# Looking up the experts' numbers with 16-bit operands, the positions spread out by ScalarE

## The chip, the cores and the metric
The kernel runs on one core of a Trainium2 chip. The time is device microseconds of one launch. [...] The engines are called PE (TensorE), DVE (VectorE), ACT (ScalarE), POOL (GpSimd) and SP (SyncE).

## The reference, cut to what matters
The layer mixes 512 latent tokens (with 256 context tokens) in an S5 group and a Hyena group, and then sends every token through PEER, an expert layer with 16384 experts that are single neurons (a row of `peer_u` and a row of `peer_v`, 1024 long). All is float32. The part of PEER that the change is in:

```python
s1, s2 = q1 @ k1.T, q2 @ k2.T            # per token and head: 128 scores each
v1, i1 = lax.top_k(s1, 16)
v2, i2 = lax.top_k(s2, 16)
cand = v1[..., :, None] + v2[..., None, :]        # 256 pairs
sc, ci = lax.top_k(cand.reshape(..., 256), 16)    # 8 heads, 16 experts a token
e = i1[ci // 16] * 128 + i2[ci % 16]              # the experts' numbers
g = softmax(sc)
act = gelu(u[e] . h)
out = sum(g * act * v[e])
```

Only 50 of the 256 pairs can be among the best 16 of a head; the kernel forms those, in a list padded to 54, with their sums `cand` and the experts' numbers `cid` beside one another.

## The kernel before, in words
Tokens are 4 blocks of 128 (`lt` 0 to 3), one token a partition. The tokens of block 0 are served by gathering their experts' rows (`gathered`, L1430 to L1439: an indirect DMA on POOL, a dot product `junk` on DVE, a gelu of one column on ACT, L1434, its product with the gate on ACT, L1436, and a weighted sum `accg` on DVE). The 384 tokens of the other blocks go through all experts as matmuls: 128 u-blocks of 128 experts (`first`: 24 matmuls of 128x384, then a gelu `ga`, stored to `GA` in DRAM, L1380) and 128 v-blocks (`second`, 18 matmuls of 128x512 into `pacc`), each weighted by a matrix of gates `GD` that is built by one-hot matmuls (`gates`, L1560). Each float32 matmul is three: an operand is split into a high part (`h`, a copy on ACT, L302, L1611, L1620) and a low part (`l`, raw minus high on DVE, L303, L1612, L1621), and L307, L308, L309 multiply high by high, low by high and high by low.

The stages after the mixers, by the trace's time:

- **Heads**, 500 to 806 us. For each of 8 heads: two query blocks `wq` (24 matmuls of 128x512 each), scores against the keys, the best 16 of both halves (`top16`), and `pairs`: the list of 54 pairs, the best 16 of them (their places in the list are `pos`), and the look-up of their experts' numbers. Between these PE does u-blocks, 6.3 a head (`run_ahead`).
- **Transition**, 806 to 832 us: the softmax over all heads, `columns` (the numbers split into two indices, transposed by PE into `ptr`, L1505 to L1507, copied by ACT into `cols`, L1514 and L1515), and `gx2`, a vector spread over partitions: eight diagonal matrices `dg` (ACT, L1573, two buffers), each multiplied by ones on PE (`pgx`, L1574).
- **Gates**, 832 to 1055 us: one-hot matrices `o` (DVE L1551, ACT L1555 and L1556), their product on PE (`pgg`), a copy to `gst` (ACT, L1562). Gathers and u-blocks lie between.
- **Last stage**, 1055 us to the end: `second` for block after block. For block i ACT makes `vh` (L1611) and `wwh` (L1620), DVE `vl` (L1612), the weights `gw` (L1617) and `wwl` (L1621). `vh`, `vl`, `wwh` and `wwl` have three buffers each, so `wwh` of block i can be written only when PE is done with block i - 3. The 37 last u-blocks and the gathers lie between.

The look-up before, per head and token block: DVE compares each of the 16 positions with the 54 numbers 0 to 53 (`eq`, 16 x 54 = 864 float32 elements a partition, L1416), multiplies by `cid` (L1417) and sums over the 54 (L1418) into `EID`.

The order of the instructions on each engine is not written out: a scheduler with a model of the durations sets it for the whole program, so that a shorter instruction in one place moves others, also in later stages. Each engine then runs its queue in that order and waits where an operand isn't there.

Of the kernel before, what the change touches and what calls it, by code (L numbers as in the profile page):

```python
# [11 lines left out]
I32 = mybir.dt.int32  # L12
BF16 = mybir.dt.bfloat16
U32 = mybir.dt.uint32
AF = mybir.ActivationFunctionType
ALU = mybir.AluOpType
AX = mybir.AxisListType

P = 128
# [74 lines left out]
RGATE = 0  # L94
PERHEAD = 0
GH = 2.0
NOO = 3
S5M = 1
HYAT = 2
# [5 lines left out]
NCAND = 54 if MERGE else 50  # L105
# [123 lines left out]
def build(tc, I, out, dbg=None, stop=None):  # L229
# [58 lines left out]
    def b2(name, shape, dtype=F32):  # L288
        return cur[0].tile(shape, dtype, tag="b2", name=name, bufs=nb2[0])
# [4 lines left out]
    def sm(name, shape, dtype=F32, bufs=1, tag=None):  # L294
        return cur[0].tile(shape, dtype, tag=tag or name, name=name, bufs=bufs)

    def wblock(src, name, lo_eng=None):
# [3 lines left out]
        lo = wp.tile([P, D], F32R, tag="wl", name=name + "l")  # L301
        nc.scalar.activation(hi, raw, AF.Copy)  # L302
        (lo_eng or (nc.vector if FQ else nc.gpsimd)).tensor_tensor(lo, raw, hi.bitcast(F32), ALU.subtract)  # L303
# [30 lines left out]
    V = nc.vector  # L334
    A = nc.scalar
# [83 lines left out]
    sc = cp.tile([P, 8, 2], F32, tag="sc", name="sc")  # L419
    A.activation(sc, ccs, AF.Silu)  # L420
    mod = cp.tile([P, 48], F32, tag="mod", name="mod")
# [15 lines left out]
    def modulated(name, rows, n, scale_c, shift_c, put, ks):  # L437
        for k in ks:
# [3 lines left out]
            hi, lo = put(k)  # L442
            A.activation(hi, pp[:, :n], AF.Identity, bias=shift_c[:, k:k + 1], scale=scale_c[:, k:k + 1])
            t = b2(f"{name}t{k}", [P, 512])[:, :n]
# [3 lines left out]
    def root_sums(n, name, ps_, diag, nb=4):  # L448
# [9 lines left out]
        def inverse(scale):  # L458
            c4 = cp.tile([P, 4], F32, tag="c4", name=name + "4", bufs=2)
            A.activation(c4[:, 0:nb], pc_[:, 0:nb], AF.Sqrt, bias=epsc, scale=scale)  # L460
            V.reciprocal(c4[:, 0:nb], c4[:, 0:nb])
# [8 lines left out]
    def row_sums(n, name, ps_, tmp, width=512):  # L470
# [4 lines left out]
        def add(t, eng=None):  # L475
            i = at[0]
            at[0] += 1
            hi, lo = (tmp(f"{name}{c}{i}", F32R)[:, 0:width] for c in "hl")
            A.activation(hi, t, AF.Copy)
            (eng or V).tensor_tensor(lo, t, hi.bitcast(F32), ALU.subtract)  # L480
# [3 lines left out]
        def inverse(scale, o, view=lambda t: t):  # L484
            root = tmp(name + "q", F32)[:, 0:width]
            A.activation(root, pc_, AF.Sqrt, bias=epsc, scale=scale)
            V.reciprocal(o, view(root))
# [848 lines left out]
    gate[0] = None  # L1336
    iota50 = sm("iota50", [P, NCAND])
    GP.iota(iota50, pattern=[[1, NCAND]], base=0, channel_multiplier=0, allow_small_or_imprecise_dtypes=True)
    iotak = sm("iotak", [P, P])
    GP.iota(iotak, pattern=[[1, P]], base=0, channel_multiplier=0, allow_small_or_imprecise_dtypes=True)  # L1340
    gt0 = rt("gt0", [P, P])
# [2 lines left out]
    EID = sm("EID", [P, 4, 8, 16])  # L1344

    def top16(val, idx, src, n, name):
        V.max(val[:, 0:8], src)
        V.max_index(idx[:, 0:8], val[:, 0:8], src)  # L1348
        rest = sm(name, [P, 128], tag="rest", bufs=4)[:, :n]
        V.match_replace(rest, val[:, 0:8], src, NEG)  # L1350
        V.max(val[:, 8:16], rest)
        V.max_index(idx[:, 8:16], val[:, 8:16], rest)  # L1352
# [22 lines left out]
    def run_ahead(share):  # L1375
        ran[0] += share
        while ran[1] < min(NRUN, ran[0]):
            i = ran[1]
            ran[1] += 1
            nc.scalar.dma_start(GA[i], first(i, V if QUIET else GP))  # L1380

    def pairs(hd, val, idx):

        if MERGE:
            V.tensor_copy(val[:, :, 4:8], idx)
            V.tensor_scalar(val[:, 0, 4:8], val[:, 0, 4:8], float(P), None, ALU.mult)
            ca = sm(f"ca{hd}", [P, 8, NCAND], tag="cand", bufs=2)
            cand, cid = ca[:, 0:4], ca[:, 4:8]
            at = 0
            for (i0, m, n) in RECTS:  # L1390
                V.tensor_tensor(ca[:, :, at:at + m * n].rearrange("p w (i j) -> p w i j", j=n), val[:, 1, :, 0:n].unsqueeze(2).broadcast_to((P, 8, m, n)),
                                val[:, 0, :, i0:i0 + m].unsqueeze(3).broadcast_to((P, 8, m, n)), ALU.add)
                at += m * n
        else:
            idf = sm(f"idf{hd}", [P, 2, 4, 16], tag="idf", bufs=2)
            V.tensor_copy(idf, idx)
            V.tensor_scalar(idf[:, 0], idf[:, 0], float(P), None, ALU.mult)
            cand = sm(f"cand{hd}", [P, 4, NCAND], tag="cand", bufs=2)
            cid = sm(f"cid{hd}", [P, 4, NCAND], tag="cid", bufs=2)
            at = 0  # L1400
            for i in range(9):
                n = 16 // (i + 1) if i < 8 else 8
                for (dst, s) in ((cand, val), (cid, idf)):
                    if i < 8:
                        V.tensor_tensor(dst[:, :, at:at + n], s[:, 1, :, 0:n], s[:, 0, :, i:i + 1].broadcast_to((P, 4, n)), ALU.add)
                    else:
                        V.tensor_tensor(dst[:, :, at:at + n], s[:, 0, :, 8:16], s[:, 1, :, 0:1].broadcast_to((P, 4, n)), ALU.add)
                at += n
        pos = sm(f"pos{hd}", [P, 4, 16], U32, tag="pos", bufs=2)
        for lt in range(4):  # L1410
            top16(SC[:, lt, hd], pos[:, lt], cand[:, lt], NCAND, f"rc{hd}{lt}")
        posf = sm(f"posf{hd}", [P, 4, 16], tag="posf", bufs=2)
        V.tensor_copy(posf, pos)
        for lt in range(4):
            eq = sm(f"eq{hd}{lt}", [P, 16, NCAND], tag="eq", bufs=2)
            V.tensor_tensor(eq, posf[:, lt].unsqueeze(2).broadcast_to((P, 16, NCAND)), iota50.unsqueeze(1).broadcast_to((P, 16, NCAND)), ALU.is_equal)  # L1416
            (GP if not QUIET and lt < EQ_POOL else V).tensor_tensor(eq, eq, cid[:, lt].unsqueeze(1).broadcast_to((P, 16, NCAND)), ALU.mult)  # L1417
            last = V.tensor_reduce(EID[:, lt, hd], eq, AX.X, ALU.add)  # L1418
        return last
# [23 lines left out]
    def softmax(hd):  # L1443
        h_ = slice(hd, hd + 1) if hd is not None else slice(0, 8)
        n = 1 if hd is not None else 8
        sc, gx = SC[:, :, h_], GX[:, :, h_]
        V.tensor_tensor(gx, sc, sc[:, :, :, 0:1].broadcast_to((P, 4, n, 16)), ALU.subtract)
        A.activation(gx, gx, AF.Exp)
        gsum = sm(f"gsum{hd}", [P, 4, 8], tag="gsum", bufs=2)[:, :, 0:n]
        V.tensor_reduce(gsum, gx, AX.X, ALU.add)  # L1450
        V.reciprocal(gsum, gsum)
        V.tensor_tensor(gx, gx, gsum.unsqueeze(3).broadcast_to((P, 4, n, 16)), ALU.mult)
        c_ = slice(16 * h_.start, 16 * h_.stop)
        V.tensor_copy(gidx[:, c_], EID[:, 0, h_].rearrange("p h k -> p (h k)"))
        V.tensor_copy(gt0[:, c_], GX[:, 0, h_].rearrange("p h k -> p (h k)"))
# [3 lines left out]
    def gathers(share, after):  # L1459
        due[0] += share  # L1460
        while due[1] < min(P, due[0]):
            gathered(due[1], after)
            due[1] += 1

    for hd in range(8):
# [12 lines left out]
        val = sm(f"val{hd}", [P, 2, 8 if MERGE else 4, 16], tag="val", bufs=2)  # L1478
        idx = sm(f"idx{hd}", [P, 2, 4, 16], U32, tag="idx", bufs=2)
        for lt in range(4):  # L1480
# [5 lines left out]
        last = pairs(hd, val, idx)  # L1486
        if PERHEAD:
            softmax(hd)
            gathers(GH if hd else 0, last)
        run_ahead(RH)  # L1490
# [27 lines left out]
    def gates_r(b_, cols, c0):  # L1518
# [3 lines left out]
        for q in range(SG // 4):  # L1522
            pg = ps.tile([P, 4, 2, P], F32, tag="pgg", name=f"pgg{b_}_{q}", bufs=2)
            t0 = c0 + 4 * q
            ts_ = slice(t0, t0 + 4)
            oo = sm(f"oo{b_}_{q}", [P, 4, 2, P], F32R, tag="oo", bufs=NOO)
            os_ = sm(f"os{b_}_{q}", [P, 4, 2, P], F32R, tag="os", bufs=NOO)
            V.tensor_tensor(oo, iotak.unsqueeze(1).unsqueeze(1).broadcast_to((P, 4, 2, P)),
# [109 lines left out]
    for i in range(P):  # L1638
# [3 lines left out]
        last = second(i, ready.pop(i, None))  # L1642
# [60 lines left out]
```

## Time and profile before
| what | value |
|---|---|
| median of 3 runs | 1772.52 us (1769.88 to 1780.96) |
| profiled execution | 1780.91 us, span 1779.1 us |
| mean granted clock | 0.977 |
| PE busy | 1669.7 us, 94% of the span |
| DVE busy | 1489.1 us, 84% |
| ACT busy | 817.7 us, 46% |
| POOL busy | 165.5 us, 9% |

Times in the trace are microseconds from the start of the span. A row of the timeline has the start, the duration, the engine, the line, the operation with its output and inputs, and in brackets for how long the engine sat idle before it and what ended that. Matmuls overlap in the records: two that follow each other without a gap start 0.17 us (128x384) or 0.23 us (128x512) apart, though each is shown as 0.33 or 0.39 us long. A wait on PE is therefore best read from the distance of two starts.

### The profile page before, as it was taken

The page shows a single profiled execution, that of the slowest core. Times are in us where ns is not written, and L with a number is a line of the kernel's source. Part 1 is how long each engine was busy: PE and PEld are TensorE (multiplying, and loading weights), DVE is VectorE, ACT ScalarE, POOL GpSimd, SP SyncE. Part 2 cuts the span into 40 slices and gives each one's busy share as a digit, 9 for nine tenths or more (in the row PEclk, how much of TensorE's full clock was granted, in tenths as well). Part 3 has the DMA queues.
Part 4 walks back from the last instruction along what each step waited for, and adds up shares of the span by engine and source line. Part 5 has one row for each costly group of instructions (what it writes and reads, how often), then busy time and mean ns, then how long its engine had stood idle before and what let it go on. Part 6 is the DMA issues. An engine that isn't in the chain of part 4 may idle for free.

```text
span 1779.1 us, 24951 instructions
## 1 busy us (share of the span) xinstructions
PE 1669.7 (94%) x8731; PEld 1410.9 (79%) x8731; DVE 1489.1 (84%) x3031; ACT 817.7 (46%) x1622; POOL 165.5 (9%) x158
## 2 busy tenths in 40 slices
PE   5799998788899999999999999989999999999997
PEld 1477655365699999999999998877778778999996
DVE  7964988986788989989999966888878888788888
ACT  3443543134443223326999864443434434444444
POOL 0000000000000000001111100111111112121222
PEclk9899999898899999999999999999999999999998
DMA  9426454131434444445988899999999999999982
GB/s 373 155 88 211 162 163 101 48 75 63 136 123 149 137 146 145 145 142 214 345 330 316 320 346 380 381 384 372 364 338 377 369 349 326 329 325 353 338 322 96
DMA packets 171092, 437.31 MB, mean 246 GB/s; under 512 B 17235, under 2 KB 102868, under 8 KB 151766
## 3 DMA queue, kind: packets, MB, share of 16 engines
q1 hardware_dynamic: 129286, 251.87, 41.8%
q0 software_dynamic: 18432, 134.23, 20.1%
q10 hardware_dynamic: 23248, 49.62, 7.8%
q8 instruction: 69, 1.13, 0.3%
q14 instruction: 57, 0.47, 0.1%
HBM read 382.11 MB, written 53.51 MB: 245 GB/s over the span
## 4 chain that ended last, share of the span: by engine, by line
PE 63%; DVE 12%; DMA 1%; issue 1%; ACT 1%; SPq 0%; DVEq 0%; ACTq 0%
PE pacc L307 10%; PE pacc L308 10%; PE pacc L309 9%; PE pa L309 6%; PE pa L307 6%; PE pa L308 6%; PE pgg L1560 5%; PE pq L309 2%; PE pq L307 2%; PE pq L308 2%; DVE idx L1352 1%; DVE rs L1350 1%; PE pg L1266 1%; DVE idx L1348 1%; DMA GD<-gst 1%
## 5 line engine op out<-in xcount | busy, mean ns | idle before, releaser
L308 PE MATMUL pacc<-vl,wwh 128*128 128x512 f32 x768 | 299.2, 390 | 0.3 <-DVE vl L1612 0.3
L309 PE MATMUL pacc<-vh,wwl 128*128 128x512 f32 x768 | 292.8, 390 | 0.0
L1430 POOL DMA_INDIRECT uvr<-in_uv_dram,gidx x128 | 153.2, 1197 | 1092.1 <-DVE accg L1439 764.2
L307 PE MATMUL pacc<-vh,wwh 128*128 128x512 f32 x768 | 241.0, 393 | 13.7 <-ACT vh L1611 13.7
L1612 DVE TENSOR_TENSOR vl<-vr,vh 128x1024 fp32r<-128x1024 f32 x128 | 155.5, 1220 | 33.3 <-ACT vh L1611 33.1
L307 PEld LDWEIGHTS pacc<-vh,wwh 128*128 128x128 f32 x768 | 144.2, 189 | 45.6 <-ACT vh L1611 16.9
L308 PEld LDWEIGHTS pacc<-vl,wwh 128*128 128x128 f32 x768 | 144.3, 188 | 30.5 <-DVE vl L1612 0.7
L309 PEld LDWEIGHTS pacc<-vh,wwl 128*128 128x128 f32 x768 | 144.2, 188 | 30.0
L1439 DVE SCALAR_TENSOR_TENSOR accg<-uvr,wgt,accg 128x1024 f32<-128x1024 f32 x128 | 163.7, 1279 | 4.5 <-ACT wgt L1436 1.9
L1611 ACT ACTIVATE vh<-vr 128x1024 fp32r<-128x1024 f32 x128 | 133.2, 1049 | 53.5 <-PE pacc L309 39.9
L1431 DVE SCALAR_TENSOR_TENSOR junk<-uvr,hrow 128x1024 f32<-128x1024 f32 x128 | 155.9, 1218 | 0.0
L1620 ACT ACTIVATE wwh<-gw 128x384 fp32r<-128x384 f32 x128 | 67.1, 524 | 183.0 <-PE pacc L308 152.1
L1621 DVE TENSOR_TENSOR wwl<-gw,wwh 128x384 fp32r<-128x384 f32 x128 | 70.8, 555 | 51.8 <-ACT wwh L1620 51.8
L1560 PE MATMUL pgg<-o,o 128*128 128x128 f32 x768 | 94.6, 275 | 0.0
L1560 PEld LDWEIGHTS pgg<-o,o 128*128 128x128 f32 x768 | 93.7, 191 | 0.0
L1551 DVE TENSOR_TENSOR o<-iotak,cols 128x512 f32<-128x512 f32 x96 | 65.9, 687 | 7.8 <-PE pgg L1560 7.6
L1434 ACT ACTIVATE wgt<-dots 128x1 f32<-128x1 f32 x128 | 25.4, 198 | 102.4 <-DVE junk L1431 102.4
L1558 DVE TENSOR_SCALAR o<-iotak,cols 128x128 f32<-128x128 f32 x240 | 70.5, 345 | 0.0
L1556 ACT ACTIVATE o<-o,cols 128x128 f32<-128x128 f32 x144 | 63.8, 494 | 0.2
L1369 ACT ACTIVATE ga<-pa 128x384 f32<-128x384 f32 x128 | 60.6, 474 | 6.0 <-PE pa L309 4.5
L1562 ACT ACTIVATE gst<-pgg 128x512 f32<-128x512 f32 x96 | 57.0, 594 | 3.1 <-PE pgg L1560 2.5
L1617 DVE TENSOR_TENSOR gw<-gal,gc 128x384 f32<-128x384 f32 x91 | 50.0, 553 | 3.4 <-DMA gal<-GA 2.8
(1811 smaller groups left out, 4136.3 us busy)
## 6 DMA issues: line engine op xcount, KB each, us to landing
vr<-in_uv_dram SPq DMA_DIRECT2D x128, 512.0 KB
GD<-gst ACTq DMA_DIRECT2D x12, 2048.0 KB
gc<-GD SPq DMA_DIRECT2D x32, 768.0 KB
GA<-ga ACTq DMA_DIRECT2D x91, 192.0 KB
gal<-GA SPq DMA_DIRECT2D x91, 192.0 KB
wb<-in_w_ada_dram SPq DMA_DIRECT2D x32, 512.0 KB
wa<-in_w_ada_dram SPq DMA_DIRECT2D x8, 1024.0 KB
KD<-kk SPq DMA_DIRECT2D x16, 256.0 KB
```

The source lines that it names most:

```text
L307: nc.tensor.matmul(o, a[0], b[0], start=start, stop=False)
L308: nc.tensor.matmul(o, a[0], b[1], start=False, stop=False)
L309: nc.tensor.matmul(o, a[1], b[0], start=False, stop=stop_)
L1430: GP.indirect_dma_start(out=uvr, out_offset=None, in_=I["uv"], in_offset=bass.IndirectOffsetOnAxis(ap=gidx[:, s:s + 1], axis=0))
L1431: ins = V.scalar_tensor_tensor(junk, uvr[:, 0:D], 1.0, hrow, ALU.mult, ALU.mult, accum_out=dots[:, s:s + 1])
L1439: V.scalar_tensor_tensor(accg, uvr[:, D:2 * D], wgt[:, s:s + 1], accg, ALU.mult, ALU.add)
L1558: last = V.tensor_scalar(o1[:, e], iotak, cols[:, 0, t:t + 1], cols[:, 2, t:t + 1], ALU.is_equal, ALU.mult)
L1560: mm = PE.matmul(pg[:, e, :], o2[:, e], o1[:, e], start=True, stop=True)
L1611: A.activation(vh, vr, AF.Copy)
L1612: (V if QUIET or i >= P - VLV else GP).tensor_tensor(vl, vr, vh.bitcast(F32), ALU.subtract)
L1620: A.activation(wh, gw, AF.Copy)
L1621: last = V.tensor_tensor(wl, gw, wh.bitcast(F32), ALU.subtract)
```

## The change
The look-up has the same three steps, with other operands. `iota16` (once) is the row 0 to 53 in bfloat16. Per head, ACT copies the experts' numbers into 16-bit integers, `cid16` (128x216). Per token block, ACT writes each position 54 times beside itself in bfloat16, `posx` (128x864, two buffers); DVE compares `posx` with `iota16`, multiplies by `cid16` and sums as before, on 16-bit operands; the sum `EID` stays float32. Line numbers grow by 1 to 4 ahead of the new block, and by 15 behind it (L303 is now L305, L1413 is L1417, L1555 is L1570, L1611 is L1626).

```diff
+iota16 = sm("iota16", [P, NCAND], BF16)
+A.activation(iota16, iota50, AF.Copy)
...
 posf = sm(f"posf{hd}", [P, 4, 16], tag="posf", bufs=2)
 V.tensor_copy(posf, pos)
+if PAIR16:
+    cid16 = sm(f"cid16{hd}", [P, 4, NCAND], I16, tag="cid16", bufs=2)
+    A.activation(cid16, cid, AF.Copy)
+    for lt in range(4):
+        posx = sm(f"posx{hd}{lt}", [P, 16, NCAND], BF16, tag="posx", bufs=2)
+        A.activation(posx, posf[:, lt].unsqueeze(2).broadcast_to((P, 16, NCAND)), AF.Copy)
+        eq = sm(f"eq{hd}{lt}", [P, 16, NCAND], I16, tag="eq", bufs=2)
+        V.tensor_tensor(eq, posx, iota16.unsqueeze(1).broadcast_to((P, 16, NCAND)), ALU.is_equal)
+        V.tensor_tensor(eq, eq, cid16[:, lt].unsqueeze(1).broadcast_to((P, 16, NCAND)), ALU.mult)
+        last = V.tensor_reduce(EID[:, lt, hd], eq, AX.X, ALU.add)
+    return last
```

The scheduler also orders the instructions differently. **DVE in head 2**, where the low part `wq6l` of a query block, for which PE waits, and the look-up (`posf` is the positions as float32) meet. Before:

```order
L1413 CAST posf2_4909<-pos2_4884 128x64
L1416 TENSOR_TENSOR eq20_4911<-posf2_4909,iota50_3927 128x864
L1416 TENSOR_TENSOR eq21_4915<-posf2_4909,iota50_3927 128x864
L303 TENSOR_TENSOR wq6l_5136<-wq6r_5133,wq6h_5135 128x1024
L1417 TENSOR_TENSOR eq20_4911<-eq20_4911,ca2_4878 128x864
```

Of the change:

```order
L1417 CAST posf2_4931<-pos2_4906 128x64
L305 TENSOR_TENSOR wq6l_5168<-wq6r_5165,wq6h_5167 128x1024
L1425 TENSOR_TENSOR eq20_4937<-posx20_4935,iota16_3929 128x864
L1426 TENSOR_TENSOR eq20_4937<-eq20_4937,cid162_4933 128x864
L1425 TENSOR_TENSOR eq21_4943<-posx21_4941,iota16_3929 128x864
```

`wq6l` has moved ahead of two of the look-up's operations; the other heads are ordered alike.

**PE behind u-block 54 in the transition**, with the transposes `ptr` and the spread vector `pgx`. Before:

```order
L309 MATMUL pa54_7233<-h2h1_3848,u54l_7230 128x384
L1574 MATMUL pgx0_7262<-dg00_7263,ones_65 128x128
L1574 MATMUL pgx0_7262<-dg01_7266,ones_65 128x128
L1574 MATMUL pgx0_7262<-dg02_7269,ones_65 128x128
L1574 MATMUL pgx0_7262<-dg03_7272,ones_65 128x128
L1505 MATMUL ptr1_7304<-ident_60,ef1_7302 128x128
L1506 MATMUL ptr1_7304<-ident_60,ef1_7302 128x128
L1507 MATMUL ptr1_7304<-ident_60,GX_3941 128x128
L1574 MATMUL pgx1_7276<-dg10_7277,ones_65 128x128
L307 MATMUL pa55_7379<-h2h0_3847,u55h_7375 128x384
```

Of the change, from the second group of transposes on:

```order
L1522 MATMUL ptr2_7399<-ident_60,GX_3943 128x128
L1520 MATMUL ptr3_7412<-ident_60,ef3_7410 128x128
L1521 MATMUL ptr3_7412<-ident_60,ef3_7410 128x128
L1522 MATMUL ptr3_7412<-ident_60,GX_3943 128x128
L1589 MATMUL pgx0_7344<-dg02_7351,ones_65 128x128
L1589 MATMUL pgx0_7344<-dg03_7354,ones_65 128x128
L1589 MATMUL pgx1_7358<-dg10_7359,ones_65 128x128
L309 MATMUL pa55_7461<-h2h0_3847,u55h_7457 128x384
```

And ACT of the change at that place, behind `u56h`, the gelu of block 54, the first `cols`, `dg02` and `dg03`:

```order
L1529 ACTIVATE cols2_7403<-ptr2_7399 128x384
L1530 ACTIVATE cols2_7403<-ptr2_7399 128x256
L1384 DMA GA_3937<-ga54_7340 128x384
L1529 ACTIVATE cols3_7416<-ptr3_7412 128x384
L1530 ACTIVATE cols3_7416<-ptr3_7412 128x256
L1570 ACTIVATE o1_0_0_7422<-iotak_3931,cols1_7390 128x128 x2
L1570 ACTIVATE o1_0_1_7443<-iotak_3931,cols1_7390 128x128
L1570 ACTIVATE o1_0_2_7491<-iotak_3931,cols1_7390 128x128 x2
L1570 ACTIVATE o1_0_3_7506<-iotak_3931,cols1_7390 128x128
L1588 ACTIVATE dg10_7359<-ident_60,mod_140 128x128
```

All three groups of transposes now stand ahead of u-block 55 (before, one), and `dg10`, for which the last `pgx` ahead of it waits, behind six one-hot operations.

**ACT in the last stage at blocks 76 to 78**. Before:

```order
L1620 ACTIVATE wwh76_12889<-gw76_12887 128x384
L1434 ACTIVATE wgt_3939<-dots_3938 128x1
L1436 ACTIVATE wgt_3939<-wgt_3939,gt0_3931 128x1
L1620 ACTIVATE wwh77_12927<-gw77_12925 128x384
L1611 ACTIVATE vh76_12881<-vr76_12877 128x1024
L1620 ACTIVATE wwh78_12959<-gw78_12957 128x384
L1611 ACTIVATE vh77_12919<-vr77_12917 128x1024
```

Of the change:

```order
L1635 ACTIVATE wwh77_13009<-gw77_13007 128x384
L1635 ACTIVATE wwh78_13041<-gw78_13039 128x384
L1626 ACTIVATE vh76_12963<-vr76_12959 128x1024
L1449 ACTIVATE wgt_3941<-dots_3940 128x1
L1451 ACTIVATE wgt_3941<-wgt_3941,gt0_3933 128x1
L1626 ACTIVATE vh77_13001<-vr77_12999 128x1024
L1626 ACTIVATE vh78_13033<-vr78_13031 128x1024
```

Here `vh76` has come to stand behind `wwh78`, two blocks on. Over blocks 0 to 87 the order of before has seven places where `vh` stands two blocks behind `wwh` in this way (at `wwh` 23, 27, 38, 46, 50, 70 and 86), and that of the change twelve (17, 19, 23, 27, 31, 42, 46, 54, 66, 70, 78 and 86).

## Rows read from the trace of the kernel before
**Rows 1.** Windows: busy us (x instructions) per engine, granted clock, DMA share, GB/s, by stage.
```profile
500.00:806.00 306.00, 302.83 (x1674) 286.63 (x1673) 270.91 (x978) 97.45 (x133) 0.00 (x0) 1.00 0.45 146
806.00:832.00 26.00, 24.54 (x142) 23.74 (x141) 25.05 (x44) 14.88 (x28) 4.23 (x3) 1.00 0.71 258
1055.00:1779.00 724.00, 695.84 (x3265) 599.42 (x3263) 587.24 (x765) 303.44 (x571) 128.15 (x107) 0.99 0.94 338
```

**Rows 2.** The tile eq: count, ns min/median/max, first and last start, forms.
```profile
L1416 DVE TENSOR_TENSOR eq<-posf,iota x32: 1042/1049/1060, 525.8 to 818.6; 128x864 f32<-128x864 f32 x32
L1418 DVE TENSOR_REDUCE EID<-eq x32: 991/1042/1050, 531.9 to 825.2; 128x16 f32<-128x864 f32 x32
```

**Rows 3.** The page's costliest groups: busy us, mean ns of one | idle before, releaser.
```profile
L1439 DVE SCALAR_TENSOR_TENSOR accg<-uvr,wgt,accg 128x1024 f32<-128x1024 f32 x128 | 163.7, 1279 | 4.5 <-ACT wgt L1436 1.9
L1611 ACT ACTIVATE vh<-vr 128x1024 fp32r<-128x1024 f32 x128 | 133.2, 1049 | 53.5 <-PE pacc L309 39.9
L1551 DVE TENSOR_TENSOR o<-iotak,cols 128x512 f32<-128x512 f32 x96 | 65.9, 687 | 7.8 <-PE pgg L1560 7.6
```

**Rows 4.** Waits of PE in the heads: total us, times, longest us.
```profile
PE pa L309 <- DVE u44l L303: 0.4, 1, 0.4
PE pq L309 <- DVE wq6l L303: 0.3, 1, 0.3
```

**Rows 5.** Timeline of PE in head 2: start us, us, instruction, [idle before <-releaser].
```profile
608.92 0.39 PE L307 MATMUL pq<-h2h,wq6h 128*128 128x512 f32 x1
609.15 0.40 PE L308 MATMUL pq<-h2l,wq6h 128*128 128x512 f32 x1
609.84 0.50 PE L309 MATMUL pq<-h2h,wq6l 128*128 128x512 f32 x1 [0.29 <-DVE wq6l L303]
610.18 0.39 PE L307 MATMUL pq<-h2h,wq6h 128*128 128x512 f32 x1
```

**Rows 6.** Timeline of DVE beside it.
```profile
606.63 2.02 DVE L1416 TENSOR_TENSOR eq<-posf,iota 128x864 f32<-128x864 f32 x2
608.57 1.22 DVE L303 TENSOR_TENSOR wq6l<-wq6r,wq6h 128x1024 fp32r<-128x1024 f32 x1
```

**Rows 7.** Timeline of PE in the transition.
```profile
825.88 0.34 PE L309 MATMUL pa<-h2h,u54l 128*128 128x384 f32 x1
...
829.32 0.45 PE L307 MATMUL pa<-h2h,u55h 128*128 128x384 f32 x1
```

**Rows 8.** Timeline of ACT in the transition.
```profile
826.07 1.06 ACT L302 ACTIVATE u56h<-u56r 128x1024 fp32r<-128x1024 f32 x1 [2.72 <-PE pa L308]
...
830.38 1.86 ACT L1555 ACTIVATE o<-iotak,cols 128x128 f32<-128x128 f32 x6
```

**Rows 9.** Timeline of PE where the last stage begins.
```profile
1077.63 0.34 PE L308 MATMUL pa<-h2l,u93h 128*128 128x384 f32 x1
1078.43 0.44 PE L309 MATMUL pa<-h2h,u93l 128*128 128x384 f32 x1 [0.46 <-DVE u93l L303]
```

**Rows 10.** Timeline of ACT at the same place.
```profile
1078.88 0.53 ACT L1620 ACTIVATE wwh<-gw 128x384 fp32r<-128x384 f32 x1 [1.57 <-DVE gw L1617]
```

**Rows 11.** Waits of PE in the last stage: total us, times, longest us.
```profile
PE pacc L307 <- ACT vh L1611: 13.7, 7, 3.6
```

**Rows 12.** Timeline of PE at the first of these waits.
```profile
1176.45 0.39 PE L309 MATMUL pacc<-vh,wwl 128*128 128x512 f32 x1
1178.17 1.66 PE L307 MATMUL pacc<-vh,wwh 128*128 128x512 f32 x6 [1.33 <-ACT vh L1611]
```

**Rows 13.** Timeline of ACT there.
```profile
1176.65 0.52 ACT L1620 ACTIVATE wwh<-gw 128x384 fp32r<-128x384 f32 x1 [1.25 <-PE pacc L308]
1177.08 1.99 ACT L1611 ACTIVATE vh<-vr 128x1024 fp32r<-128x1024 f32 x2
```

**Rows 14.** Timeline of PE at the dearest of them.
```profile
1299.39 2.93 PE L307 MATMUL pacc<-vh,wwh 128*128 128x512 f32 x6 [3.63 <-ACT vh L1611]
```

**Rows 15.** Windows right behind that wait.
```profile
1299.00:1303.00 4.00, 3.61 (x10) 2.89 (x11) 4.00 (x4) 2.24 (x3) 1.68 (x1) 0.59 1.06 373
```

More of the change, by code (lines that the diff above doesn't have):

```diff
@@ L14 @@
 U32 = mybir.dt.uint32
+I16 = mybir.dt.int16
 AF = mybir.ActivationFunctionType
@@ L96 @@
 GH = 2.0
+PAIR16 = 1
 NOO = 3
```

## The prediction
> **What bounds the kernel now.** I read four views in this order. First the busy time of each engine by stage: in the heads PE is busy for 302.8 of 306 us, though DVE with 270.9 is near it, and ACT with 97.5 has two thirds of its time free; in the 26 us of transition PE and DVE are both nearly full; in the last stage PE does 695.8 of 724 us [rows 1]. So PE sets the time, and the look-up, which is DVE's work, counts only where PE waits for something that stands behind it in DVE's queue. Second the durations of the look-up [rows 2]. Third the waits of PE, to see which of them hang on DVE or ACT [rows 4, 11]. Fourth the timelines around these waits, for the price of one [rows 5 to 10, 12 to 15]. Last I laid the orders of the two programs beside these places, since the scheduler's new durations move instructions in stages that the edit does not touch.
>
> **What it removes on DVE.** The look-up is 32 comparisons and 32 products of 1.049 us and 32 sums of 1.042 us [rows 2], 100 us in all. The comparisons and products now have 16-bit operands, which no row of before shows. Bounds: no gain (1.05 us), or two elements a step, 432 steps instead of 864. A product of two operands took 0.687 us at 512 elements [rows 3] and 1.049 at 864 [rows 2], which is 1.03 ns an element; at 432 that is 0.60 us. I take 0.60, since all tensors of both are 16-bit and contiguous along the 54. That is 64 x 0.45 = 29 us less on DVE. The sum I leave at 1.04, as its result stays float32. [...]
>
> Of these 29 us, PE gets back only what it waits for. In the heads it waits seven times for a low part that DVE makes late, 0.3 to 0.4 us each [rows 4]. Head 2 shows one: two comparisons, 606.63 to 608.65, stand ahead of wq6l on DVE [rows 6]; PE starts the matmul on wq6l 0.69 us after the one before it instead of 0.23, and the next 0.34 later [rows 5], so the place costs 0.46 + 0.11 = 0.57 us. Where the wait is 0.4 [rows 4] I add 0.1: two of 0.67 and five of 0.57 make **-4.2 us**. In the new order the low part stands directly behind posf, two operations earlier, and this goes whole. Next late would be the following low part (wq7l); between posf and it stand wq6l and two comparisons, two products and a sum, 4 x 0.60 + 1.04 = 3.4 us; before, wq6l and four such operations of 1.05, 4.2 us. So it is earlier than before, when PE did not wait for it.
>
> **What it adds on ACT.** 32 spreads of 864 elements: a copy of 1024 took 1.049 us [rows 3], so 0.89 us each, 28 us; 8 copies of 216 and one of 54 are under 0.4 us each, 3 us in all. ACT has 306 - 97 = 209 us free in the heads [rows 1], and its waits are for PE. I cost it at nothing. Its cover is that slack; where a spread stands ahead of a high part that PE needs next, it would cost up to 0.89 us at that place. A first spread also delays the first comparison; nothing but EID waits for that, and the low part has passed it.
>
> **Transition.** Ahead of u52l on DVE now also stand a reciprocal, a product of 128x512, a sum of the look-up and a copy of gates. That is 1.04 [rows 2] + 0.69 [rows 3] + two small ones, which I put at 0.3 each: 2.3 us. Four look-up operations there give 1.8 back, so u52l is some 0.5 us later, and PE already waits for it: **+0.6** (0 to +2.4, the upper end if 16-bit gives nothing).
>
> Then PE. It finishes u-block 54 with the matmul of 825.88 and starts u-block 55 at 829.32 [rows 7]. Now the last product ahead of u-block 55 needs dg10, behind six one-hot operations on ACT, which ended at 830.38 + 1.86 = 832.24 with the same high part u56h ahead at 826.07 [rows 8]. What ACT has ahead of them changes in kind (two more pairs of cols for four operations of gx2) and hardly in length. So u-block 55 starts near 832.2, **+2.9 us**, with PE idle. The other three operands of that vector stand among further one-hot work: from nothing (PE has matmuls of u-block 55 to do meanwhile) to another 1.86 us [rows 8]; I take +0.6, for the six transposes done early are given back. Together +3.5, with 0 to +5 as ends.
>
> **Start of the last stage.** Before, PE did 21 matmuls of u-block 93 ahead of block 0, the second ending at 1077.97 and a wait of 0.46 us in front of the third [rows 9]. The new order has only two of them there, and then needs wwh of block 0, which ACT ended at 1079.41 [rows 10]: a wait of 1.44 in place of 0.46, **+1.0** (0 to +3).
>
> **Last stage.** Here lies the largest term, and nothing in it was edited. wwh has three buffers, so ACT can write that of block j only when PE is done with j - 3. Where vh of j - 2 stands behind it on ACT, PE has nothing to do until both are done. Before, PE waits 13.7 us in seven waits for vh [rows 11], and the order of before has exactly seven such places. The first: PE's last matmul of a block starts at 1176.45 [rows 12], ACT, released by it, makes wwh at 1176.65 and then vh from 1177.08 [rows 13], and PE goes on at 1178.17: 1.72 - 0.23 = 1.49 us. [...] All seven cost 13.7 + 7 x 0.16 (the restart, 1.49 - 1.33) + 1.4 + some 0.4 for late vl: 16.6. The new order has twelve places. At none of them does a dot product stand behind wwl with its gelu ahead of vh, so all are of the cheap kind: 12 x 1.49 = 17.9. At four to five of them DVE has a weighted sum, 1.28 us [rows 3], or the like ahead of vl, of which I count 0.9: 4.4 in all. 17.9 + 4.4 - 16.6 = **+5.7** (0, if the extra places find PE with other work as one of before near block 90 does; +12, if each is 2.4).
>
> **Sum.** -4.2 + 0.6 + 3.5 + 1.0 + 5.7 = +6.6 us. The profiled execution of 1780.91 would become 1787.5; it is 8.4 us above the median of the runs, so I put the change on the median: 1772.5 + 6.6 = **1779 us**. One per cent is 17.7 us, about what a measurement can tell from no change.
>
> **Rivals.**
>
> - *The new order costs nothing.* Only the waits in the heads go, the added places in the transition and the last stage are covered, as their engines may run ahead of the queue I assume. 1772.5 - 4.2 = 1768. For it: of eight places in the old order one costs nothing. Against it: the other seven cost what the mechanism says.
> - *The dear kind of place in the last stage, and slower.* The gathers shift by a few us, and dot products reach DVE only with wwl already queued ahead of them. Then a place costs 3.63 + 0.16 = 3.8 us [rows 14] and twelve cost 45.5, 28.9 more than now: 1772.5 - 4.2 + 0.6 + 3.5 + 1.0 + 28.9 = 1802. It decides from the point where DVE ends the dot product later than wwl at more than half of the places. Against it: two of seven were so before, and in the new order the dot product stands ahead of wwl wherever a gelu lies between.
> - *16-bit gives nothing.* Comparisons and products stay at 1.05 us. The low parts two behind in a head then come late by some 0.8 us (a queue of 4 x 1.05 + 1.04 against my 3.4, 1.8 longer, less about 1 that the low part now has in hand by standing earlier), 6.4 over eight heads, u52l by 2.4: -4.2 + 6.4 + 2.4 + 3.5 + 1.0 + 5.7 = +14.8, 1787. For it: no row has a 16-bit two-operand instruction. [...] Against it, by the rows alone: even then the heads have DVE at 271 of 306 us as now, so most of its price hangs on single places; I give it little.
> - *DVE bounds the heads after all.* Then the whole 29 us come off: 1744. Against it: PE's waits for DVE there sum to a few us [rows 1, 4].
>
> **How the numbers follow.** Forecast 0.62, nothing for the order 0.22, the dear kind 0.07, 16-bit without gain 0.06, DVE as the bound 0.03. Range: from 1768 less the 2.6 us by which the lowest run of before lies under its median, 1766, up to the upper ends of the order's terms (+5 for the transition, +3, +12 would add up to 1789) and the third rival: 1790. That leaves out the second and fourth rivals and tails of the first. Faster by over 1% (under 1754.8): 0.03. Slower by over 1% (over 1790.2): the dear kind and a tail of the others, 0.09. Within: 0.88.
>
> **What would show it.** In the changed profile: comparisons and products of about 0.60 us and a sum still of 1.04; DVE's busy time in the heads near 242 us, ACT's near 128, PE's stage no shorter than by 4 us; no wait of PE there for wq4l, wq6l and their like; u-block 55 starting about 6 us behind the last matmul of u-block 54; twelve waits of PE for vh in the last stage, of 1.3 us mostly, some 18 us in all. The prediction is wrong if these waits are longer than 2 us on average, if they are seven or fewer, or if the heads shorten by tens of us.

## The result, and the profile after

Six runs of the changed kernel took 1786.64 us in the median (1785.22 to 1790.74), six of the kernel before 1772.52 (1769.88 to 1780.96): a ratio of 1.0073, 95% interval [1.0055, 1.0092]. The change costs 14 us between the medians, 0.7 to 0.8%: slower, clear of noise, and about twice the 6.6 us that the prediction summed. The time lies within its range (1766 to 1790) and within the 1% on either side to which it gave 0.88. One per cent was said to be about what a measurement can tell; the interval here is 0.2% to each side. The profiled execution of the changed kernel took 1787.44 us.

The windows of the changed kernel, by stage (columns as in [rows 1]):

```profile
500.00:806.00 306.00, 305.51 (x1693) 291.43 (x1693) 254.57 (x989) 127.34 (x175) 2.06 (x1) 1.00 0.45 149
806.00:832.00 26.00, 22.29 (x132) 21.83 (x131) 18.80 (x43) 16.55 (x42) 5.42 (x4) 0.87 0.70 263
1055.00:1785.00 730.00, 693.64 (x3226) 592.36 (x3224) 584.29 (x763) 299.80 (x567) 138.51 (x107) 0.99 0.93 332
```

The tiles of the look-up, which answer to [rows 2], and the spread:

```profile
L1425 DVE TENSOR_TENSOR eq<-posx,iota x32: 596/601/610, 518.4 to 804.7; 128x864 int16<-128x864 bf16 x32
L1426 DVE TENSOR_TENSOR eq<-eq,cid x32: 594/600/609, 519.0 to 805.9; 128x864 int16<-128x864 int16 x32
L1427 DVE TENSOR_REDUCE EID<-eq x32: 1040/1045/1053, 520.1 to 807.5; 128x16 f32<-128x864 int16 x32
...
L1423 ACT ACTIVATE posx<-posf x32: 905/913/925, 517.4 to 801.0; 128x864 bf16<-128x864 f32 x32
```

Every price of the edit itself came out: 0.60 us for comparison and product, 1.045 for the sum, 0.913 for the spread (0.89 was estimated). DVE's busy time fell from 1489.1 to 1461.2 us over the span, 28 us for the 29 forecast. (In the window of 500 to 806 us it is 254.6 and not the 242 given as a sign, because the heads start 8.5 us earlier in this trace and the window holds some of the work behind them; from the first query matmul to u-block 51 it fell from 283.2 to 259.0.) The kernel as a whole gained no time from it. What PE got and lost stands in the starts of its instructions, stage by stage. Heads means from the first query matmul (the start of wq0) to u-block 51; transition and gates from there to u-block 88; last stage from there to PE's last matmul; each from one profiled execution:

| kernel | heads | transition and gates | last stage |
|---|---|---|---|
| before, first profile | 321.8 | 246.1 | 711.4 |
| before, second profile (first experiment) | 322.2 | 246.1 | 714.1 |
| changed | 318.2 | 251.5 | 725.1 |

Against the first profile: heads -3.7, transition and gates +5.4, last stage +13.7 (+11.0 against the second profile). The places, as the forecast named them:

**Heads.** PE at the low part of head 2 [rows 5], and DVE ahead of it [rows 6]:

```profile
599.79 0.40 PE L310 MATMUL pq<-h2l,wq6h 128*128 128x512 f32 x1
600.03 0.40 PE L311 MATMUL pq<-h2h,wq6l 128*128 128x512 f32 x1
```

```profile
597.00 0.20 DVE L1417 CAST posf<-pos 128x64 f32<-128x64 uint32 x1
597.12 1.22 DVE L305 TENSOR_TENSOR wq6l<-wq6r,wq6h 128x1024 fp32r<-128x1024 f32 x1
598.26 0.60 DVE L1425 TENSOR_TENSOR eq<-posx,iota 128x864 int16<-128x864 bf16 x1
```

0.24 us between the two starts in place of 0.69: no wait is left.

**Transition.** PE at the end of u-block 54 and the start of 55 [rows 7], ACT beside it [rows 8], and the window behind:

```profile
814.18 0.34 PE L311 MATMUL pa<-h2h,u54l 128*128 128x384 f32 x1
...
816.81 0.78 PE L1589 MATMUL pgx<-dg,ones 128*128 128x128 f32 x4 [0.86 <-ACT dg L1588]
820.43 0.79 PE L1589 MATMUL pgx<-dg,ones 128*128 128x128 f32 x2 [2.84 <-ACT dg L1588]
820.92 0.69 PE L309 MATMUL pa<-h2h,u55h 128*128 128x384 f32 x1
```

```profile
818.20 1.89 ACT L1570 ACTIVATE o<-iotak,cols 128x128 f32<-128x128 f32 x6
819.95 0.42 ACT L1588 ACTIVATE dg<-ident,mod 128x128 f32<-128x128 f32 x1
```

```profile
820.40:826.20 5.80, 5.77 (x18) 5.77 (x19) 3.69 (x8) 3.62 (x11) 0.60 (x1) 0.50 0.29 116
```

dg10 waits behind six one-hot operations and PE behind it, as forecast: 814.18 to 820.92 is 6.74 us, where the text said about 6. What it did not price is the stretch behind: for 5.8 us after the idle time PE ran at a granted clock of 0.50 (1.00 is the full one), and that is 2.9 us of its own.

**Last stage.** PE's waits there, which answer to [rows 11], and one of them [rows 12]:

```profile
PE pacc L309 <- ACT vh L1626: 16.7, 12, 1.8
PE pa L309 <- ACT ga L1373: 4.5, 1, 4.5
PE pacc L310 <- DVE vl L1627: 3.7, 5, 0.8
```

```profile
1150.34 0.39 PE L311 MATMUL pacc<-vh,wwl 128*128 128x512 f32 x1
1152.06 0.73 PE L309 MATMUL pacc<-vh,wwh 128*128 128x512 f32 x2 [1.33 <-ACT vh L1626]
```

Twelve waits for vh, none of the dear kind (at its wait of 3.63 us [rows 14] the kernel before has a gelu on ACT between wwh and vh, and ACT sat idle for 1.77 us until its dot product `junk` was there), and the price of one is again 1152.06 - 1150.34 - 0.23 = 1.49 us. Counted by PE's 18 matmuls a block, they stand in front of blocks 15, 17, 21, 25, 29, 40, 44, 52, 64, 68, 76 and 84: each two blocks ahead of one of the twelve places in ACT's order, and at no other block. The seven waits of before stand the same way to its seven places.

The second line of the waits is the start of the stage: PE's starts, ACT's queue and the clock there, to be held against [rows 9, 10]:

```profile
1068.74 0.34 PE L311 MATMUL pa<-h2h,u92l 128*128 128x384 f32 x1
1073.56 0.69 PE L309 MATMUL pa<-h2h,u93h 128*128 128x384 f32 x1 [4.48 <-ACT ga L1373]
1074.05 0.52 PE L310 MATMUL pa<-h2l,u93h 128*128 128x384 f32 x1
1074.57 0.77 PE L309 MATMUL pacc<-vh,wwh 128*128 128x512 f32 x1
```

```profile
1070.70 0.33 ACTq L1384 DMA_DIRECT2D GA<-ga  x1
1071.13 1.06 ACT L1626 ACTIVATE vh<-vr 128x1024 fp32r<-128x1024 f32 x1 [9.07 <-DMA gal<-GA]
```

```profile
1073.50:1078.00 4.50, 4.44 (x10) 3.29 (x11) 4.50 (x7) 3.33 (x6) 0.00 (x0) 0.50 1.11 374
```

PE stood 4.65 us (start to start, less 0.17) in front of u-block 93, and then ran at 0.50 again; ACT had stood still for 9 us at the store of block 90's gelu, the last one that is stored. The kernel before has the same two waits, only shorter:

```profile
1077.35 0.44 PE L307 MATMUL pa<-h2h,u93h 128*128 128x384 f32 x1 [1.45 <-ACT ga L1369]
```

```profile
1074.92 1.06 ACT L1611 ACTIVATE vh<-vr 128x1024 fp32r<-128x1024 f32 x1 [6.04 <-DMA gc<-GD]
```

### The profile page after: what moved, and what is told of

It reads as the page before. It is cut to its first block, busy times and chain, and to the rows that moved or that the text cites. A ratio compares the mean times of both kernels' runs of the same rounds, so it can differ in the third digit from the quotient of the medians.

```text
span 1785.7 us, 24989 instructions
## 1 busy us (share of the span) xinstructions
PE 1671.6 (94%) x8731; PEld 1410.9 (79%) x8731; DVE 1461.2 (82%) x3031; ACT 844.4 (47%) x1663; POOL 176.1 (10%) x158
## 4 chain that ended last, share of the span: by engine, by line
PE 71%; DVE 2%; DMA 1%; ACT 1%; issue 1%; SPq 0%; ACTq 0%; DVEq 0%
PE pacc L310 10%; PE pa L309 10%; PE pa L311 10%; PE pa L310 10%; PE pacc L311 9%; PE pacc L309 9%; PE pgg L1575 5%; PE pq L309 2%; PE pq L310 2%; PE pq L311 2%; PE pg L1268 1%; PE psc L1498 1%; DMA GD<-gst 1%; PE po L309 1%; PE po L310 1%
## 5 line engine op out<-in xcount | busy, mean ns | idle before, releaser
L1445 POOL DMA_INDIRECT uvr<-in_uv_dram,gidx x128 | 163.8, 1280 | 1092.4 <-DVE accg L1454 764.1
L309 PE MATMUL pacc<-vh,wwh 128*128 128x512 f32 x768 | 234.9, 394 | 16.7 <-ACT vh L1626 16.7
L1626 ACT ACTIVATE vh<-vr 128x1024 fp32r<-128x1024 f32 x128 | 133.2, 1049 | 40.5 <-PE pacc L311 30.3
L1570 ACT ACTIVATE o<-iotak,cols 128x128 f32<-128x128 f32 x144 | 52.3, 403 | 0.0
```

The source lines that it names most:

```text
L309: nc.tensor.matmul(o, a[0], b[0], start=start, stop=False)
L1445: GP.indirect_dma_start(out=uvr, out_offset=None, in_=I["uv"], in_offset=bass.IndirectOffsetOnAxis(ap=gidx[:, s:s + 1], axis=0))
L1626: A.activation(vh, vr, AF.Copy)
```

## The experiments

Each time is the median of its runs; the kernel before, run beside them, had medians of 1772 to 1775 us. Stages are those of the table above.

**The kernel before, profiled again.** No edit.

> The kernel before, profiled a second time. Theory: the 8.4 us by which its first profiled execution lies above the median were spent ahead of the heads, in work that the change does not touch (the first query block started at 487.0 us there and at 478.5 us in the changed kernel, with the same instructions ahead of it). Then this execution, if it takes about 1772 us, starts the first query block near 478.5 us and is within 1 us of the first profile from there to the end of each stage; seven waits of PE for vh again. Rival: the 8.4 us lie in the last stage (its two dear waits of 3.5 and 3.8 us are absent in an ordinary execution); then the start is at 487 again and the vh waits sum to 9 to 10 us instead of 13.7.

One run, 1771.14 us. The start of the first query block in the first profile of before, in this one, and in the changed kernel:

```profile
487.02 0.77 PE L307 MATMUL pq<-h2h,wq0h 128*128 128x512 f32 x1
```

```profile
474.16 0.80 PE L307 MATMUL pq<-h2h,wq0h 128*128 128x512 f32 x1
```

```profile
478.47 0.80 PE L309 MATMUL pq<-h2h,wq0h 128*128 128x512 f32 x1
```

The theory held for the place of the 8.4 us, and the spread ahead of the heads is wider than thought: 474 to 487 us in two executions of the same kernel. The first profile of before was a late starter, which is why 1787.4 less 1780.9, the 6.5 us between the two profiled executions, looks like the forecast and is not its proof; from the first query matmul to the end of the span the change costs 15.1 us against the first profile and 12.0 against the second. The last stage of this second profile was 2.7 us longer, where at most 1 was expected: its waits for vh are the same seven, but behind that of 3.31 us (3.30 in the first profile, with a clock of 1.00 from 1198 to 1202 us) the clock was 0.50 here:

```profile
1185.43 0.80 PE L307 MATMUL pacc<-vh,wwh 128*128 128x512 f32 x1 [3.31 <-ACT vh L1611]
```

```profile
1185.00:1189.00 4.00, 3.56 (x8) 2.84 (x9) 3.58 (x4) 2.46 (x4) 0.89 (x1) 0.50 0.89 337
```

**The changed kernel, and the kernel before, with one rule for ACT's order in the last stage.** ACT may write wwh of a block only after vh of the block before it (called vh first from here on). Both get these lines in `second`:

```diff
-        A.activation(vh, vr, AF.Copy)
+        vhs.append(A.activation(vh, vr, AF.Copy))
...
-        A.activation(wh, gw, AF.Copy)
+        iw = A.activation(wh, gw, AF.Copy)
+        if i >= 1:
+            tc.add_manual_dep(iw.ins, vhs[i - 1].ins.name, NOSYNC, ...)
```

> The changed kernel, in which only the order on ACT in the last stage is set: wwh of block i stands behind vh of block i-1, so none of the twelve places is left. Theory (buffers and order): the twelve waits of PE for vh (18.6 us from start to start) and most of the five for vl (4.8) vanish: 1786.6 - 18 to 23 = 1764 to 1769 us. Rival (the waits cover for something else, such as late rows or late weights): they come back as waits for wwh, wwl or the loads, and the time stays above 1780.

1762.15 us (1760.35 to 1765.39), 0.9927 of the kernel before [0.9902, 0.9951], 2 us under the range of the theory. The last stage shrinks from 725.1 to 697.8 us, and no wait for vh, vl, wwh or wwl is left. What PE still waits for from 800 us on:

```profile
PE pa L309 <- ACT ga L1373: 4.2, 2, 4.0
PE pgx L1589 <- ACT dg L1588: 3.7, 2, 2.8
PE pa L311 <- DVE u52l L305: 0.3, 1, 0.3
```

> The kernel before with the same one rule for ACT's order in the last stage. Theory: its seven waits (15 to 17 us) vanish too, so 1772.5 - 15 = 1757 us, 1755 to 1761, and the difference between it and the changed kernel with the same rule shrinks from 14 us to what the other stages give: -3.9 (heads) + 5.4 (transition) + 7 (start of the last stage) = 8 to 9. Rival (the last stage's order is not what the change costs): the difference between the two stays 14 us.

1756.38 us (1755.16 to 1758.15), 0.9901 [0.9875, 0.9926]. Last stage 693.7 us. Between the two kernels under the rule 5.8 us are left of 14 (8 to 9 were expected): heads -2.6, transition +4.4, last stage +4.1, which sums to 5.9. So some 8 us of the change's 14 lay in ACT's order in the last stage (five more places, and vl late behind some of them). The rule that takes them away leaves the look-up as it is.

**Four buffers for wwh and wwl in the changed kernel, no rule for the order.** In both lines of `second`, `bufs=NVH` (three) becomes 4.

> The changed kernel with no rule for the order, but four buffers for wwh and wwl instead of three (vh and vl keep three). The scheduler now lets ACT run further ahead with wwh: at 49 blocks vh of two blocks back stands behind wwh, at nine blocks even vh of three blocks back. Theory (a place costs only where the buffer that wwh needs comes free with the block just before the one whose vh is still to be made): with four buffers the 49 cost nothing, and the nine cost 1.5 us each, 13 us, with a few us of late vl: 1786.6 - 23 + 13 to 18 = 1777 to 1782 us, with nine waits of PE for vh. Rival (vh standing two blocks behind costs by itself): 58 waits and 1786.6 + 46 x 1.5 = 1855.

1781.77 us (1779.15 to 1784.07), 1.0046 [1.0029, 1.0063]. Waits of PE in the last stage:

```profile
PE pacc L309 <- ACT vh L1626: 12.8, 11, 1.4
PE pa L309 <- ACT ga L1373: 4.9, 1, 4.9
PE pacc L310 <- DVE vl L1627: 2.3, 3, 0.8
```

Of 58 blocks whose vh stands two or three back, nine cost 1.49 to 1.58 us each, and two more 0.3 and 0.5. The nine waits stand in front of blocks 25, 29, 36, 40, 51, 59, 67, 79 and 83, each three blocks ahead of one of the nine places where vh stands three back. The mechanism is the buffer together with the order, not the order by itself.

**Eight buffers for dg.** `bufs=2` becomes 8, in the changed kernel and in the kernel before, each with vh first.

> The changed kernel with vh first as in the run before it, and eight buffers for the diagonal matrices dg in place of two, so that ACT makes them all long before the transition and none of PE's products there waits behind the one-hot work. Theory: the 3.7 us of waits for dg and the half clock behind them (PE at 0.50 of its clock for some 5 us, about 2.9 us) go: 5 to 6 us under the run with vh first alone, unless the start of the last stage, where the order changes too (no matmul of u-block 93 ahead of block 0 instead of two), takes some of it back. Rival (the transition is bound by DVE's and ACT's softmax work): no more than 1 us.

1755.30 us (1751.42 to 1758.73), 6.9 us under the run with vh first alone. Transition and gates take 244.5 us for 250.5, with no wait for dg and, from 805 to 840 us, a clock of 1.00: in the trace the wait and the half clock behind it were worth the 5 to 6 us expected. The last stage, whose start has another order here, takes 694.0 us for 697.8 besides, so that the 6.9 us of the runs do not price the transition alone.

> The kernel before with vh first in the last stage and eight buffers for dg, that is the two rules of the last run without the edit itself. Its order at the start of the last stage comes out as the changed kernel's (two matmuls of u-block 93 ahead of block 0 instead of 21, and ACT's store of the gelu of block 90 takes the completion semaphore that the load of gal1 had, not that of gc0). Theory (the start of the last stage costs what its order makes it, whatever the look-up): about 4 us more there than in the kernel before with vh first, less 1.2 us of waits for dg: 1756.4 + 4 - 1.2 = 1759 us. Rival (the longer wait at that start comes from the new look-up): 1755.

1767.70 us (1763.95 to 1771.41), 9 us more than expected. The term that it was built for came: the last stage is 697.5 us against 693.7, with a wait of 4.4 us where the kernel before with vh first alone had 1.7:

```profile
PE pa L307 <- ACT ga L1369: 4.4, 1, 4.4
```

So the long wait at that start comes with the order, and the old look-up has it too. The rest is a wait that was not forecast: with dg early, PE waited 4.09 us for a one-hot matrix of the gates, and the granted clock was 0.64 from 832 to 840 us; transition and gates take 251.4 us for 246.1.

```profile
832.64 1.65 PE L1560 MATMUL pgg<-o,o 128*128 128x128 f32 x6 [4.09 <-ACT o L1556]
```

**The last store by POOL**, in the changed kernel with vh first:

```diff
-            nc.scalar.dma_start(GA[i], first(i, ...))
+            (nc.gpsimd if i == NRUN - 1 else nc.scalar).dma_start(GA[i], first(i, ...))
```

> The changed kernel with vh first, in which the store of the gelu of block 90 (the last one stored) is issued by POOL, not by ACT. Theory: in the changed kernel ACT's queue stood still behind that store for 8 us at the start of the last stage, because the store waits for the semaphore of an earlier load; with the store elsewhere vh of block 0 and u93h come earlier, PE's wait of 4.0 us there falls to 2 or less and with it the half clock behind it: 1762 - 2 to 6 = 1756 to 1760 us. Rival: vh of block 0 itself waits until the loads of block 0 have landed, so the wait stays at 4 us and the time at 1762.

The profile agrees with the theory: PE's waits in the last stage are

```profile
PE pacc L309 <- ACT wwh L1637: 1.4, 1, 1.4
PE pacc L309 <- issue: 0.8, 1, 0.8
```

the clock stays at 1.00 there, and the stage takes 693.8 us for 697.8. The runs do not: 1762.55 us (1758.16 to 1764.69), as without it and as the rival had it. What took the 4 us back in the runs is not settled; the spread ahead of the heads is wider than they are.

**The two halves of the edit.** First 16-bit operands without the spread (`posf` in bfloat16, read in place), with vh first:

> The changed kernel with vh first, without the spread by ACT: posf is cast to bfloat16 by DVE, and the comparison reads each position 54 times in place. Products as in the change. [...] For the time: the comparisons stand ahead of the low part again, so PE's waits for it in the heads are back (4 us if 1.05 us each, 1 to 2 if 0.60); no one-hot work stands ahead of dg10, so the transition costs 3 to 5 us less than in the change. Near 1762 either way.

1761.15 us (1757.69 to 1762.68), and:

```profile
L1423 DVE TENSOR_TENSOR eq<-posf,iota x32: 1043/1051/1059, 513.7 to 805.6; 128x864 int16<-128x864 bf16 x32
L1424 DVE TENSOR_TENSOR eq<-eq,cid x32: 595/601/606, 516.7 to 808.5; 128x864 int16<-128x864 int16 x32
```

The comparison is back at 1.05 us: with 16-bit operands, but each position read 54 times in place, it takes what it took in float32, while the product, which reads a row of 54 numbers 16 times, takes 0.60. On the spread positions the comparison of the changed kernel took 0.60 as well: of 16-bit operands, it was the spread that brought it down here. The heads take 321.9 us, as before, and the waits for low parts are back (PE pq for wq6l 0.2 us, and six like it). Transition and gates take 247.5 us, 4 less than in the change, as expected, though PE still waits 1.8 us for dg.

Then the spread alone, in float32, with vh first:

```diff
-                posx = sm(..., [P, 16, NCAND], BF16, tag="posx", bufs=2)
+                posx = sm(..., [P, 16, NCAND], F32, tag="posx", bufs=2)
...
-                eq = sm(..., [P, 16, NCAND], I16, tag="eq", bufs=2)
+                eq = posx
```

> The changed kernel with vh first, in which ACT spreads the positions but all operands stay float32 (the comparison writes over the spread positions, as two more buffers of that size do not fit). Comparisons and products take 1.05 us as before; the low part stands ahead of them as in the change; the transition and the start of the last stage come out ordered as in the kernel before. Theory (what the heads gain is the place of the low part in DVE's queue, not the 16-bit rate): the heads are 2 to 4 us shorter than in the kernel before, and the time is 1756.4 - 3 = 1753 us, 1751 to 1757. Rival (the rate does it): low parts come late behind the slower operations, and the heads take as long as before or longer: 1757 to 1763.

1751.15 us (1748.02 to 1753.21), 0.9865 [0.983, 0.9901], which is 11 us under the 16-bit look-up with the same rule. By the traces 1.6 us of that lie in the heads, 5.1 in transition and gates and 2.3 in the last stage, where the order came out differently. DVE in head 2:

```profile
593.80 0.19 DVE L1417 CAST posf<-pos 128x64 f32<-128x64 uint32 x1
593.91 1.22 DVE L305 TENSOR_TENSOR wq6l<-wq6r,wq6h 128x1024 fp32r<-128x1024 f32 x1
595.05 2.02 DVE L1425 TENSOR_TENSOR posx<-posx,iota 128x864 f32<-128x864 f32 x2
```

The heads take 317.5 us with operations of 1.05 us, no longer than with 0.60: the gain there is the place of the low part in the queue. That place goes with the spread: with it, in 16 bits or in float32, the low part stands ahead of the comparisons, and without it, in the run before this one, behind them. That the scheduler does so because the first comparison has to wait for ACT is argued and not tried.

**Everything at once, in float32 and in 16 bits.** Spread, vh first, eight dg buffers and the store by POOL:

> The run with the spread in float32 and vh first, with eight buffers for dg and the last store of a gelu by POOL besides. Theory: the transition loses its 1.3 us of waits for dg and the start of the last stage its wait of 2.2 us with the half clock behind it (1.6): 1751 - 2 to 4 = 1747 to 1750 us. Rival (the new order elsewhere gives it back, as in the kernel before with vh first and eight buffers): 1751 to 1758.

1749.82 us (1748.70 to 1756.69), 0.9874 [0.9856, 0.9893]: within the theory's range, but not apart from the run without the last two rules, though in the trace transition and gates are 1.7 us shorter than there and the last stage 2.9.

> The changed kernel as it is, 16-bit look-up and all, with the three rules of the last run: vh first, eight buffers for dg, the last store by POOL. It differs from the run before it only in that the look-up's operands are 16-bit and not float32. Theory (the rate of the look-up is worth nothing where PE does not wait for it): the same time, 1748 to 1754 us, with the heads within 1 us of 317 and the other stages within 1 us too. Rival (the 29 us less on DVE pay once the order is out of the way): 1740 us or less.

1751.28 us (1750.49 to 1753.55), 0.9883 [0.9867, 0.9899]. Windows over 300 us of the heads, float32 first, then 16-bit:

```profile
500.00:800.00 300.00, 300.00 (x1669) 286.66 (x1668) 273.61 (x985) 125.47 (x171) 0.00 (x0) 1.00 0.44 148
```

```profile
500.00:800.00 300.00, 300.00 (x1665) 286.66 (x1664) 248.68 (x986) 124.01 (x171) 0.00 (x0) 1.00 0.45 148
```

25 us less work on DVE, and PE is full in both: the heads differ by 1.8 us, the wrong way (317.0 and 318.8; within 1 was expected). With these rules in both kernels the 16-bit operands are worth nothing that can be measured. Both, and the spread in float32 with vh first alone, are 1.2 to 1.4% faster than the kernel before. How far the spread takes these beyond the kernel before with vh first (1.0%, 0.9901 [0.9875, 0.9926]) the intervals do not tell.

## Why the prediction was right, and what it mis-sized

The engine that bounds was read rightly: PE sets the time, and a look-up that is 28 us shorter on DVE changes it only through PE's waits. The direction and the places were right; the size was not, since 14 us came for 6.6, and only the width of the range covers that. Term by term:

- *Heads, -4.2*: -3.7. The waits for low parts went as forecast; the float32 spread shows that it was their place.
- *16-bit at 0.60 us, sum at 1.04, ACT for nothing*: 0.60, 1.045, and 27 us more on ACT over the span (817.7 to 844.4) that PE did not wait for.
- *Transition, +0.6 and +3.5*: +5.4 for 4.1. The waits for dg were right: u-block 55 starts 6.74 us behind the last matmul of 54, where it had been 3.44. The step that failed is "u-block 55 starts near 832.2, +2.9 us, with PE idle", which left out the stretch behind the idle time: 5.8 us at a clock of 0.50, 2.9 us. The sum counts 1.4 us for such a stretch in the last stage, and I did not carry that over. The six transposes that now stand ahead of u-block 55 give some 0.7 us back.
- *Start of the last stage, +1.0 (0 to +3)*: +5.2, outside its own bounds, and the step that failed most. I read a wait for wwh and for an order of 21 or two matmuls. ACT's queue in fact stood at a store, and PE in front of u-block 93 for its buffer, which the gelu behind the same store sets free: 4.65 us where the two waits at that place had been 2.24 (1.61 and 0.63), and 2.8 us of half clock (5.5 us at 0.50). The first of these two waits of before, 1.61 us, was in the trace and went unread.
- *Last stage, +5.7*: the twelve waits for vh cost 18.6 us from start to start, the late vl 4.6, together 23.2 for 22.3 forecast. Against the 16.6 that the waits of before were put at, that is +6.6. No run shows the 1.4 us that these 16.6 count for the clock behind the dearest wait of before; [rows 15] show a granted clock of 0.59 over 4 us with PE busy for 3.61 of them, some 1.5 us by my estimate (3.61 x 0.41). Besides, some 2 us more of the stage's 13.7 were not traced to a wait. The mechanism is shown by taking it away in both kernels, and by the fourth buffer.
- *The median*: the sum was put on the median, which was right, since the first profile's 8.4 us lie ahead of all of this. The terms then should have added up to the 14 us of the runs, and came to 6.6.

The rivals: "the new order costs nothing" fell (twelve waits, two for dg). The dear kind did not occur (the longest wait for vh was 1.8 us). "16-bit gives nothing" fell: the operations took 0.60 us, and in the heads no low part came late. That its 1787 us is the time that was measured is luck, as what it had over the forecast was mainly for such late parts. DVE as the bound fell.

## What to carry to other kernels

In a program whose order a scheduler sets, an edit that shortens instructions on an engine that is not the bound is above all an edit of that order. List the places where the bounding engine waits on a buffer or a queue in the old order and in the new one, price them by the waits already in the trace, and add the clock that PE loses behind a wait wherever the trace shows it. Where such a place costs, fix the order by a rule of one line (make vh before the next wwh): here that was worth 1% in the kernel before and 1.4% in the changed one, while the faster look-up was worth nothing. Look at the whole order again after each such rule: eight buffers for dg took 7 us off the changed kernel with vh first, and added 11 to the kernel before with vh first. And profile a kernel twice before taking the difference of two traces as the change.

## What the runs showed that was not expected

- PE's wait did not tell by its length alone whether the clock falls. In the changed kernel a wait of 2.84 us (for dg) was followed by 5.8 us at a granted clock of 0.50, one of 4.48 us (for ga, at the start of the last stage) by 5.5 us at 0.50, and one of 1.75 us (for vh) by 1.00 from 1198.5 to 1201 us. A wait of 3.3 us was followed by 0.50 from 1185 to 1189 us in one execution of the kernel before and by 1.00 from 1198 to 1202 us in another, with the same instructions. So the price of such a wait had two values here.
- ACT stood 9.07 us at one store in the changed kernel and 6.04 in the kernel before. The profile names a load as what let it go on: of gal in the changed kernel, of the gates gc in the kernel before. Moving the store to POOL took PE's wait of 4.0 us for ga away in the trace. That the store waits there because it shares a completion semaphore with that load, and that the order of the DMAs decides which load it is, is my reading of the program and was not shown by a run.
